# Scale and shift of a pre-norm moved from row operands to column operands, in a two-layer fp32 encoder

## The chip, the cores and the metric

One NeuronCore of a Trainium2 chip runs the whole program. The metric is device microseconds of one execution; the figure of a kernel is the median of several. In the profile the engines are PE (TensorE's matmuls), PEld (its weight loads), DVE (VectorE), ACT (ScalarE), POOL (GpSimd) and SP (SyncE, which issues the transfers).

## The reference

Two layers, 512 tokens, width 1024, fp32. Each layer has two sub-layers (a token mixer of four head groups, then a SwiGLU feed-forward of width 2816), each wrapped in the same way:

```
def _rms_norm(x, g, eps=RMS_EPS):
    y = xf * lax.rsqrt(jnp.mean(xf * xf, axis=-1, keepdims=True) + eps)
    return (y * g.astype(jnp.float32)).astype(x.dtype)

# per sub-layer, with shift, scale, gate taken from c by a linear layer:
h = _rms_norm(x, g_pre) * (1 + scale) + shift
x = x + gate * _rms_norm(sublayer(h), g_post)
```

So between two sub-layers, a token's row y of the finished sub-layer is normed, multiplied by a gate that differs per feature, added to x; the new x is normed again, multiplied per feature by S = (1 + scale) g_pre, and shifted per feature by H = shift. Gate, S and H depend on the feature and not on the token.

## The kernel before

Each fp32 product is made of three matmuls on parts: an operand is split into hi (rounded to the type fp32r) and lo (the rest), and mm3 issues hi·hi (L192), hi·lo (L193) and lo·hi (L194). The activations that feed a GEMM are kept transposed in hT: hT[:, 0] is hi, hT[:, 1] is lo, features on the 128 partitions in eight chunks kc, tokens along the row.

Between two sub-layers lies a **boundary**, in four tiles of 128 tokens, T0 to T3. There are four: b0 (mixer of layer 0 to its FFN, some 320 to 375 us into the span), b1 (FFN of layer 0 to the mixer of layer 1, some 715 to 765 us), b2 (mixer of layer 1 to its FFN, some 1000 to 1055 us) and a last one at the end, which has only the gate. The GEMM before a boundary leaves a tile's row y in two PSUM banks of 512 features each. boundary_tile then squares and sums the banks (L291 on ACT) and multiplies them by the gate row G (L293 on DVE); computes 1/rms from a few one-column instructions; adds the residual (L299); squares again (L303); and makes yt = x · r2 · S + H in two halves (L312 on DVE, then L313, the first half on POOL and the second on DVE). G, S and H are tiles in which one row of 1024 features is repeated on all 128 partitions. make_rows computes them as columns (rcol, 24 columns of 128 features), and cols_to_rows transposes them and writes them to DRAM; boundary_start reads them back as rows, 512 KB each, into three tiles of the pool FS. What remains of FS goes into the boundary's ring of buffers.

The function transposed() of a tile runs later: PE transposes yt in eight pieces of 128x128 (L319) back into the tile's own two banks, and split makes hi (L205, ACT) and lo (L206, DVE) from each bank of 512 columns, both reading the bank.

The next GEMM (FFN or mixer) can use T0 and T1 before T2 and T3 are there: it runs first on the tokens 0 to 255 (matmuls of 256 columns), the transposes of T2 and T3 are placed in between, then on the tokens 256 to 511. In b1 the 448-column value part (v_part, 48 matmuls of tokens 0 to 255) lies between T3's transposes and the first matmul that needs T3.

A scheduler orders the instructions of each engine when the kernel is built. Each engine executes its list in order, and an instruction that waits holds up what is behind it.

Of the kernel before, what the change touches and what calls it, by code (L numbers as in the profile page):

```python
# [16 lines left out]
A = mybir.AluOpType  # L17
AF = mybir.ActivationFunctionType
AX = mybir.AxisListType

L, D, T, FF = 2, 1024, 512, 2816
# [70 lines left out]
def f(ap):  # L92
    return ap.bitcast(F32)
# [3 lines left out]
def hybrid_encoder(ctx: ExitStack, tc: tile.TileContext, x_in, c_in, pos_in, cols_in, rows_in, ktab_in, wada, wz, wst,  # L97
# [5 lines left out]
    act, dve, pool, pe, sync = nc.scalar, nc.vector, nc.gpsimd, nc.tensor, nc.sync  # L103
# [3 lines left out]
    def persist(name, shape, dt=F32):  # L107
        t = sb.tile(shape, dt, name=name)
        tags[id(t)] = name
        return t  # L110
# [8 lines left out]
    hT = persist("hT", [128, 2, KC, T], F32R)  # L119
# [3 lines left out]
    FS = Pool2([persist(f"f{i}", [128, 1024]) for i in range(8)])  # L123
# [5 lines left out]
    rcol = persist("rcol", [128, 24])  # L129
# [10 lines left out]
    def small(n=1):  # L140
        s = state["s"]
        if s + n > 128:
            s = 0
        state["s"] = s + n
        return sml[:, s:s + n]

    x_mid = [dr.tile([T, D], F32, name=f"xmid{i}") for i in range(2 * L)]
    rows_d = [dr.tile([24, 128], F32, name=f"rowsd{i}") for i in range(2 * L)]
# [6 lines left out]
    def dram_ap(t, offset, ap):  # L155
        a = t[:] if not isinstance(t, bass.AP) else t
        return bass.AP(tensor=a.tensor, offset=a.offset + offset, ap=ap)
# [46 lines left out]
    def split(hi, lo, src):  # L204
        act.activation(hi, src, AF.Copy)  # L205
        dve.tensor_tensor(lo, src, f(hi), A.subtract)  # L206
# [7 lines left out]
    def col(l, c, n=8):  # L214
        return cols[:, l, c:c + n]

    def modcol(l, part):
        return mod[:, l, part * 8:part * 8 + 8]

    def add_bias(l, part):  # L220
        dve.tensor_tensor(modcol(l, part), modcol(l, part), col(l, C_BADA + part * 8), A.add)

    def make_rows(idx, ps, gate, pre):

        l, part, g = gate
        add_bias(l, part)
        dve.tensor_tensor(rcol[:, 0:8], modcol(l, part), col(l, g), A.mult)
        if pre:
            l, psc, psh, g = pre
            add_bias(l, psc)  # L230
            add_bias(l, psh)
            dve.scalar_tensor_tensor(rcol[:, 8:16], modcol(l, psc), 1.0, col(l, g), A.add, A.mult)
            dve.tensor_copy(rcol[:, 16:24], modcol(l, psh))
        n = 24 if pre else 8
        cols_to_rows(rcol[:, 0:n], n, rows_d[idx], ps)

    def rsqrt_col(ss, n):
        r = small()
        act.activation(r, ss, AF.Sqrt, bias=epst[:], scale=1.0 / n)
        dve.reciprocal(r, r)  # L240
        return r
# [12 lines left out]
    def cols_to_rows(c, n, d, ps):  # L254

        tmp = RAW.get()
        pe.transpose(ps[0:n, 0:128], c, ident[:])
        act.activation(tmp[0:n, 0:128], ps[0:n, 0:128], AF.Copy)
        sync.dma_start(d[0:n, :], tmp[0:n, 0:128])
        RAW.put(tmp)  # L260

    def boundary_start(idx, src, pre):
        st = {"idx": idx, "src": src, "pre": pre}
        names = ("G", "S", "H") if pre else ("G",)
        for i, nme in enumerate(names):
            st[nme] = FS.full()
            sync.dma_start(st[nme][:], dram_ap(rows_d[idx], i * D, [[0, 128], [1, D]]))
        st["scr"] = FS.half()
        st["junk"] = st["scr"][:, 0:256].bitcast(BF16)
        st["own"] = [FS.full() for _ in range(min(4, len(FS.full_free)))]  # L270
        st["raw"] = [RAW.get(), RAW.get()]
        st["ring"] = Ring(st["own"] + st["raw"] + ([cact] if idx else []))
        return st

    def boundary_end(st):
        for nme in ("G", "S", "H") if st["pre"] else ("G",):
            FS.put(st[nme])
        for t in st["own"]:
            FS.put(t)
        RAW.put(*st["raw"])  # L280
        FS.put_half(st["scr"])

    def boundary_tile(st, t, y, dst):

        xt, yt = st["ring"].get(), st["ring"].get()
        rows = slice(t * 128, t * 128 + 128)
        sync.dma_start(xt[:], st["src"][rows, :])
        ss = small(4)
        for e in range(2):
            h = slice(e * 512, e * 512 + 512)  # L290
            act.activation(st["junk"], y[e][:], AF.Square, accum_out=ss[:, e:e + 1])  # L291
            h = slice((1 - e) * 512, (1 - e) * 512 + 512)
            dve.tensor_tensor(yt[:, h], y[1 - e][:], st["G"][:, h], A.mult)  # L293
        s1 = small()
        dve.tensor_tensor(s1, ss[:, 0:1], ss[:, 1:2], A.add)
        r1 = rsqrt_col(s1, D)
        for e in range(2):
            h = slice(e * 512, e * 512 + 512)
            dve.scalar_tensor_tensor(xt[:, h], yt[:, h], r1, xt[:, h], A.mult, A.add)  # L299
            if not st["pre"] and t == NT - 1:  # L300
                sync.dma_start(dst[rows, h], xt[:, h])
            if st["pre"]:
                act.activation(st["junk"], xt[:, h], AF.Square, accum_out=ss[:, 2 + e:3 + e])  # L303
        if st["pre"] or t < NT - 1:
            sync.dma_start(dst[rows, :], xt[:])
        if st["pre"]:
            s2 = small()
            dve.tensor_tensor(s2, ss[:, 2:3], ss[:, 3:4], A.add)
            r2 = rsqrt_col(s2, D)
            for e in range(2):  # L310
                h = slice(e * 512, e * 512 + 512)
                dve.scalar_tensor_tensor(yt[:, h], xt[:, h], r2, st["S"][:, h], A.mult, A.mult)  # L312
                (pool, dve)[e].tensor_tensor(yt[:, h], yt[:, h], st["H"][:, h], A.add)  # L313
        st["ring"].put(xt)

        def transposed():
            for e in range(2):
                for k in range(4):
                    pe.transpose(y[e][:, k * 128:k * 128 + 128], yt[:, e * 512 + k * 128:e * 512 + k * 128 + 128], ident[:])  # L319
                src = y[e][:].rearrange("p (k t) -> p k t", k=4)  # L320
                split(hT[:, 0, e * 4:e * 4 + 4, rows], hT[:, 1, e * 4:e * 4 + 4, rows], src)
            st["ring"].put(yt)

        st[t] = transposed
# [306 lines left out]
    def mixer(l, tile2=None):  # L631
# [55 lines left out]
        else:  # L687
            zb, vb = [bank[i] for i in (0, 4, 1, 5)], [bank[i] for i in (2, 6, 3, 7)]
            us = env.pop("us") + [load_unit(wst[l, kc], 960, True) for kc in range(EARLY, KC)]
            for half in range(2):  # L690
                for j in range(4):
                    for kc in range(KC):
                        z_part(zb[j], us[kc], j, kc, half * 256, half * 256 + 256)
                    if half == 0 and j == 0:
                        tile2(0)[0][2]()
                if half == 0:
                    tile2(0)[0][3]()
                    boundary_end(tile2(0)[0])
                for t in (2 * half, 2 * half + 1):
                    for kc in range(KC):  # L700
                        v_part(vb[t], us[kc], t, kc)
# [500 lines left out]
    def ffn(l, yb, st, us, rows, tile2):  # L1202
# [14 lines left out]
        for half in range(2):  # L1217
            for n, (ug, uu, pg, pu) in enumerate(us):
                gemm_z(pg, ug, half * 256, half * 256 + 256)
                if half == 0 and n == 0:  # L1220
                    st[2]()
                gemm_z(pu, uu, half * 256, half * 256 + 256)
            if half == 0:
                st[3]()
                boundary_end(st)
# [30 lines left out]
    for l in range(L):  # L1256
        b = L * 4 + l * 128
        lam_init = 0.8 - 0.6 * math.exp(-0.3 * l)
        e = small(2)
# [47 lines left out]
    src = x_in  # L1307
    for l in range(L):
# [3 lines left out]
        st = {}  # L1312

        def rows1():
            make_rows(2 * l, yb[3][1], (l, 2, C_GQM), (l, 4, 3, C_GPF))
            st.update(boundary_start(2 * l, src, True))

        def tile1(t):
            boundary_tile(st, t, yb[t], dst)
# [10 lines left out]
        src2, src = dst, out if last else x_mid[2 * l + 1]  # L1330
        st2 = {}

        def tile2(t, l=l, src2=src2, src=src, st2=st2, last=last):
            if not st2:
                st2.update(boundary_start(2 * l + 1, src2, not last))
            return st2, t, (bank[t], bank[4 + t]), src

        ffn(l, yb, st, us, lambda ps: make_rows(2 * l + 1, ps, (l, 5, C_GQF), None if last else (l + 1, 1, 0, C_GPM)), tile2)


# [79 lines left out]
```

## Time and profile before

| | us |
|---|---|
| median of 3 runs | 1412.16 (1410.44 to 1414.13) |
| profiled execution | 1408.21 |
| its span, first to last instruction | 1406.4 |
| PE busy | 1316.7 (94%) |
| DVE busy | 822.9 (59%) |
| ACT busy | 609.2 (43%) |
| POOL busy | 157.4 (11%) |

The span covers one execution from its first to its last instruction; busy time is what an engine's instructions took, overlapped ones counted once. The mean clock granted to TensorE was 0.976 of full speed.

### The profile page before, as it was taken

How to read it: one execution, taken by the hardware profiler on the slowest of the kernel's cores; microseconds unless marked ns; L12 is line 12 of the kernel's file. 1: busy time of each engine (PE TensorE's matmuls, PEld its weight loads, DVE VectorE, ACT ScalarE, POOL GpSimd, SP SyncE). 2: the span in 40 equal slices, each digit the busy share in tenths (PEclk: the TensorE clock that was granted, in tenths of full speed). 3: DMA queues.
4: the chain of work that ended last, by engine and by line, in shares of the span. 5: the costliest groups of instructions: out<-in, count | busy, mean ns of one | idle time of the engine just before them, and what ended most of it. 6: DMA issues, size and time to landing. Idle time of an engine off the chain costs nothing. (4 is left out here: it accounts for less than half of the span.)

```text
span 1406.4 us, 17870 instructions
## 1 busy us (share of the span) xinstructions
PE 1316.7 (94%) x6512; PEld 1090.2 (78%) x6512; DVE 822.9 (59%) x1562; ACT 609.2 (43%) x1163; POOL 157.4 (11%) x156
## 2 busy tenths in 40 slices
PE   4989899899999999999989998999989999999998
PEld 4857777677888887778869787777878888888886
DVE  6969887886665556542274597778574333332223
ACT  6555555765422222232252575677543223232212
POOL 0223332111000000000031112211010000000000
PEclk9989899999999999999999999999999999999999
DMA  8776786736476666663344533653553233323321
GB/s 314 258 193 205 256 255 207 220 114 222 147 245 215 215 217 226 225 225 90 105 139 143 150 108 107 181 152 109 183 175 120 90 105 90 105 105 125 100 90 60
DMA packets 80324, 231.69 MB, mean 165 GB/s; under 512 B 11276, under 2 KB 12268, under 8 KB 80236
## 3 DMA queue, kind: packets, MB, share of 16 engines
q1 hardware_dynamic: 80236, 230.55, 51.1%
q8 instruction: 51, 0.84, 0.2%
q14 instruction: 37, 0.30, 0.1%
HBM read 188.85 MB, written 14.40 MB: 145 GB/s over the span
## 5 line engine op out<-in xcount | busy, mean ns | idle before, releaser
L192 PE MATMUL bank<-hT,w 128*128 128x512 f32 (+1 forms) x992 | 376.3, 381 | 12.6 <-ACT hT L1299 4.0
L194 PE MATMUL bank<-hT,w 128*128 128x512 f32 (+1 forms) x992 | 376.7, 380 | 4.1 <-DVE w L183 3.3
L193 PE MATMUL bank<-hT,w 128*128 128x512 f32 (+1 forms) x992 | 377.4, 381 | 2.1 <-DVE hT L206 2.1
L178 ACT ACTIVATE w<-r 128x1024 fp32r<-128x1024 f32 (+1 forms) x132 | 138.4, 1056 | 329.1 <-PE bank L194 111.1
L183 DVE TENSOR_TENSOR w<-r,w 128x1024 fp32r<-128x1024 f32 (+1 forms) x102 | 124.5, 1222 | 238.1 <-ACT w L178 238.1
L192 PEld LDWEIGHTS bank<-hT,w 128*128 128x128 f32 x992 | 189.6, 192 | 48.2 <-ACT w L178 4.9
L194 PEld LDWEIGHTS bank<-hT,w 128*128 128x128 f32 x992 | 190.2, 192 | 40.1 <-DVE w L183 6.3
L193 PEld LDWEIGHTS bank<-hT,w 128*128 128x128 f32 x992 | 190.2, 192 | 34.8 <-DVE hT L206 2.9
L192 PE MATMUL bank<-w,r 128*128 128x512 f32 (+1 forms) x312 | 122.2, 392 | 1.6 <-DVE r L206 0.8
L194 PE MATMUL bank<-w,r 128*128 128x512 f32 (+1 forms) x312 | 121.2, 389 | 1.1 <-DVE r L206 1.1
L193 PE MATMUL bank<-w,r 128*128 128x512 f32 (+1 forms) x312 | 120.7, 387 | 0.0
L178 ACT ACTIVATE w<-raw 128x1024 fp32r<-128x1024 f32 (+1 forms) x48 | 50.3, 1051 | 121.4 <-PE bank L194 42.6
L211 DVE SCALAR_TENSOR_TENSOR r<-r,cact 128x1024 f32<-128x1024 f32 x69 | 84.6, 1227 | 28.4 <-DMA r<-in_wada_dram 27.4
L485 PE MATMUL bank<-ident,f 128*128 128x128 f32 x464 | 76.0, 285 | 11.4 <-DVE f L461 4.5
L205 ACT ACTIVATE r<-bank 128x512 fp32r<-128x512 f32 (+3 forms) x121 | 61.2, 513 | 48.9 <-PE bank L485 31.9
L183 DVE TENSOR_TENSOR w<-raw,w 128x1024 fp32r<-128x1024 f32 (+1 forms) x38 | 46.1, 1213 | 55.4 <-ACT w L178 55.4
L485 PEld LDWEIGHTS bank<-ident,f 128*128 128x128 f32 x464 | 55.3, 145 | 27.6 <-ACT f L440 7.5
L192 PEld LDWEIGHTS bank<-w,r 128*128 128x128 f32 x312 | 58.7, 188 | 15.7 <-DVE r L206 1.4
L194 PEld LDWEIGHTS bank<-w,r 128*128 128x128 f32 x312 | 58.7, 188 | 13.4 <-DVE r L206 1.6
L206 DVE TENSOR_TENSOR r<-bank,r 128x512 fp32r<-128x512 f32 (+3 forms) x89 | 49.9, 568 | 32.0 <-ACT r L205 31.6
L180 POOL TENSOR_TENSOR w<-r,w 128x512 fp32r<-128x512 f32 (+1 forms) x30 | 45.2, 1505 | 208.9 <-ACT w L178 156.9
L193 PEld LDWEIGHTS bank<-w,r 128*128 128x128 f32 x312 | 58.8, 188 | 11.5
(399 smaller groups left out, 2171.4 us busy)
## 6 DMA issues: line engine op xcount, KB each, us to landing
r<-in_wada_dram SPq DMA_DIRECT2D x69, 512.0 KB
r<-in_wgu_dram SPq DMA_DIRECT2D x66, 512.0 KB
r<-in_wdn_dram SPq DMA_DIRECT2D x33, 512.0 KB
raw<-in_wada_dram SPq DMA_DIRECT2D x27, 512.0 KB
raw<-in_wgu_dram SPq DMA_DIRECT2D x22, 512.0 KB
r<-r SPq DMA_DIRECT2D x35, 256.0 KB
r<-in_wz_dram SPq DMA_DIRECT2D x17, 512.0 KB
r<-w SPq DMA_DIRECT2D x66, 128.0 KB
```

The lines of the kernel that those rows point to most:

```text
L178: act.activation(hi[:, :w], raw[:, :w], AF.Copy)
L180: pool.tensor_tensor(lo[:, :w // 2], raw[:, :w // 2], f(hi[:, :w // 2]), A.subtract)
L183: dve.tensor_tensor(lo[:, :w], raw[:, :w], f(hi[:, :w]), A.subtract)
L192: pe.matmul(ps, a[0], b[0], start=start, stop=False)
L193: pe.matmul(ps, a[0], b[1], start=False, stop=False)
L194: pe.matmul(ps, a[1], b[0], start=False, stop=stop)
L205: act.activation(hi, src, AF.Copy)
L206: dve.tensor_tensor(lo, src, f(hi), A.subtract)
L211: dve.scalar_tensor_tensor(raw[:], raw[:], 1.0, cact[:], A.mult, A.mult, accum_out=mod[:, l, e:e + 1])
L485: pe.transpose(tb[:, s], P[:, s], ident[:])
```

## The change

Only G goes to DRAM and comes back as a row: 8 columns instead of 24 are transposed, and one row tile of 512 KB is loaded per boundary instead of three. The two tiles of FS that held S and H join the boundary's ring. boundary_tile now makes yt = x · r2 in one instruction of 1024 columns. S and H are applied after the transposes, when features lie on partitions: per piece of 128 columns, ACT writes hi = bank · s + h straight from the bank (s and h are columns of rcol), DVE computes the same value in fp32 from the bank into the buffer yt, and per 512 columns one more DVE instruction subtracts hi from it to give lo.

```diff
-        n = 24 if pre else 8
-        cols_to_rows(rcol[:, 0:n], n, rows_d[idx], ps)
+        cols_to_rows(rcol[:, 0:8], 8, rows_d[idx], ps)
...
-        names = ("G", "S", "H") if pre else ("G",)
-        for i, nme in enumerate(names):
-            st[nme] = FS.full()
-            sync.dma_start(st[nme][:], dram_ap(rows_d[idx], i * D, [[0, 128], [1, D]]))
+        st["G"] = FS.full()
+        sync.dma_start(st["G"][:], dram_ap(rows_d[idx], 0, [[0, 128], [1, D]]))
...
-            for e in range(2):
-                h = slice(e * 512, e * 512 + 512)
-                dve.scalar_tensor_tensor(yt[:, h], xt[:, h], r2, st["S"][:, h], A.mult, A.mult)
-                (pool, dve)[e].tensor_tensor(yt[:, h], yt[:, h], st["H"][:, h], A.add)
+            dve.tensor_scalar(yt[:], xt[:], r2, None, A.mult)
...
-                src = y[e][:].rearrange("p (k t) -> p k t", k=4)
-                split(hT[:, 0, e * 4:e * 4 + 4, rows], hT[:, 1, e * 4:e * 4 + 4, rows], src)
+                for k in range(4 * e, 4 * e + 4):
+                    ps, s, h = y[e][:, (k % 4) * 128:(k % 4) * 128 + 128], rcol[:, 8 + k:9 + k], rcol[:, 16 + k:17 + k]
+                    act.activation(hT[:, 0, k, rows], ps, AF.Identity, bias=h, scale=s)
+                    dve.tensor_scalar(yt[:, k * 128:k * 128 + 128], ps, s, h, A.mult, A.add)
+                dve.tensor_tensor(hT[:, 1, e * 4:e * 4 + 4, rows], yt[:, e * 512:e * 512 + 512].rearrange("p (k t) -> p k t", k=4),
+                                  f(hT[:, 0, e * 4:e * 4 + 4, rows]), A.subtract)
```

Line numbers of the changed kernel that the prediction uses: the scaling by r2 is L306; PE's transposes are L312; ACT's pieces are L315, DVE's L316, the subtraction L317; the old L293 is L289 and the old L299 is L295.

The scheduler lists the instructions anew. On DVE, at the end of T3 in b0 (its banks are bank_66 and bank_70; f_108 and f_111 are buffers of yt), before:

```order
L312 SCALAR_TENSOR_TENSOR f_108<-raw_102,sml,f_107 128x512 x2
L313 TENSOR_TENSOR f_108<-f_108,f_110 128x512
L206 TENSOR_TENSOR hT<-bank_66,hT 128x4x128
L206 TENSOR_TENSOR hT<-bank_70,hT 128x4x128
L183 TENSOR_TENSOR w_73<-r_163,w_72 128x1024
```

and after the change, from T3's L306 on, which stands among T2's pieces (f_110 and bank_69 are T2's), with the waits that the program holds in brackets (the waiting semaphore's number left as printed):

```order
L306 TENSOR_SCALAR f_111<-f_108,sml 128x1024 [waits DVE_49]
L316 TENSOR_SCALAR f_110<-bank_69,rcol 128x128 [waits Activation_49] x3
L317 TENSOR_TENSOR hT<-f_110,hT 128x4x128 [waits DVE_49]
L316 TENSOR_SCALAR f_111<-bank_66,rcol 128x128 [waits Activation_49]
L316 TENSOR_SCALAR f_111<-bank_70,rcol 128x128 [waits Activation_49]
L316 TENSOR_SCALAR f_111<-bank_66,rcol 128x128 [waits Activation_49]
```

Five more L316 follow, the two banks still in turn, and then T3's two L317: the two instructions behind T3's transposes became ten. Each L316 waits for ACT, as the brackets show, although it reads nothing that ACT writes; in ACT's list each L315 but the first of a bank waits for DVE in the same way. The two engines go through a bank piece by piece in turn, on two banks at once.

On PE, where the first GEMM behind b0 begins, T1's transposes (banks 64 and 68) are followed before by the GEMM, with T2's transposes (bank_65) 49 matmuls later:

```order
L319 MATMUL bank_64<-ident,f_108 128x128 x4
L319 MATMUL bank_68<-ident,f_108 128x128 x4
L192 MATMUL bank_63<-hT,w_72 128x256
L192 MATMUL bank_67<-hT,w_75 128x256
L193 MATMUL bank_63<-hT,w_72 128x256
```

and after the change T2's eight stand ahead of the GEMM's first L193:

```order
L312 MATMUL bank_64<-ident,r_165 128x128 x4
L312 MATMUL bank_68<-ident,r_165 128x128 x4
L192 MATMUL bank_63<-hT,w_72 128x256
L192 MATMUL bank_67<-hT,w_75 128x256
L312 MATMUL bank_65<-ident,f_110 128x128 x4
L312 MATMUL bank_69<-ident,f_110 128x128 x4
L192 MATMUL bank_64<-hT,w_1589 128x256
L193 MATMUL bank_63<-hT,w_72 128x256
```

T2's transposes moved ahead; in b2 it is the same, and in b1 T2's eight and four of T3's stand there. T3's eight stay behind some 94 matmuls of 256 columns in b0 and b2.

On DVE in b1, the work ahead of T1's L317 (which the mixer's first L193 waits for) now holds the pieces of T0 and T1, and some of T2's chain; this is its middle part (f_109 is T1's buffer, r_165 T2's, cact and r_2919 T3's):

```order
L289 TENSOR_TENSOR r_2919<-bank_66,f_108 128x512
L317 TENSOR_TENSOR hT<-r_2920,hT 128x4x128
L316 TENSOR_SCALAR r_2920<-bank_67,rcol 128x128
L291 TENSOR_TENSOR sml<-sml 128x1
L316 TENSOR_SCALAR f_109<-bank_64,rcol 128x128
L317 TENSOR_TENSOR hT<-r_2920,hT 128x4x128
L239 RECIPROCAL sml<-sml 128x1
L316 TENSOR_SCALAR f_109<-bank_68,rcol 128x128
L295 SCALAR_TENSOR_TENSOR cact<-r_2919,sml,cact 128x512
L295 SCALAR_TENSOR_TENSOR cact<-r_2919,sml,cact 128x512
L316 TENSOR_SCALAR f_109<-bank_64,rcol 128x128
```

T3's L289 and L295, the old L293 and L299, now stand between T1's pieces.

## Rows read from the trace of the kernel before

**Rows 1.** The page: span and busy time of each engine.

```profile
span 1406.4 us, 17870 instructions
PE 1316.7 (94%) x6512; PEld 1090.2 (78%) x6512; DVE 822.9 (59%) x1562; ACT 609.2 (43%) x1163; POOL 157.4 (11%) x156
```

**Rows 2.** Groups of PE by shape: busy us, mean ns, idle before, its releasers.

```profile
L319 PE MATMUL bank<-ident,f 128*128 128x128 f32 x48 | 7.2, 281 | 5.1 <-POOL f L313 3.9 <-DVE sml L240 1.1
L319 PE MATMUL bank<-ident,r 128*128 128x128 f32 x40 | 5.9, 274 | 1.0 <-POOL r L313 1.0
```

**Rows 3.** Timeline of PE in b0, b1, b2: start, us, instruction, [idle before <-releaser].

```profile
350.25 1.34 PE L319 MATMUL bank<-ident,f 128*128 128x128 f32 x8 [1.36 <-POOL f L313]
352.97 0.58 PE L193 MATMUL bank<-hT,w 128*128 128x256 f32 x1 [0.87 <-DVE hT L206]
...
369.70 1.27 PE L319 MATMUL bank<-ident,f 128*128 128x128 f32 x8 [1.66 <-POOL f L313]
371.77 0.38 PE L193 MATMUL bank<-hT,w 128*128 128x256 f32 x1
...
737.58 0.80 PE L192 MATMUL bank<-hT,r 128*128 128x256 f32 x2 [2.73 <-ACT hT L205]
...
1030.40 1.32 PE L319 MATMUL bank<-ident,cact 128*128 128x128 f32 x8 [0.30 <-POOL cact L313]
...
1035.37 0.58 PE L193 MATMUL bank<-hT,w 128*128 128x256 f32 x1 [1.26 <-DVE hT L206]
```

**Rows 4.** Windows: length, busy PE, PEld, DVE, ACT, POOL, clock, DMA share, GB/s.

```profile
718.50:738.20 19.70, 14.95 (x70) 11.40 (x68) 17.96 (x30) 10.92 (x30) 6.22 (x4) 0.91 0.20 70
353.00:359.00 6.00, 6.00 (x28) 6.00 (x29) 4.44 (x11) 3.19 (x10) 0.76 (x1) 0.50 0.22 87
1030.00:1035.40 5.40, 1.91 (x12) 1.17 (x11) 5.00 (x10) 3.19 (x8) 0.34 (x1) 0.96 0.29 83
1035.40:1038.40 3.00, 3.00 (x14) 3.00 (x15) 2.36 (x6) 1.08 (x5) 0.77 (x1) 0.51 0.56 227
```

**Rows 5.** Groups of ACT by shape.

```profile
L291 ACT ACTIVATE f<-bank 128x512 bf16<-128x512 f32 x24 | 14.2, 593 | 33.1 <-DVE r L293 30.2 <-PE bank L194 1.7 <-DVE f L293 0.9
L334 ACT ACTIVATE r<-bank 128x512 fp32r<-128x512 f32 x9 | 5.3, 592 | 4.1 <-DVE w L206 1.9 <-issue 1.3 <-PE bank L415 0.7
L334 ACT ACTIVATE r<-bank,kcst 128x512 fp32r<-128x512 f32 x5 | 3.4, 687 | 4.7 <-PE bank L194 4.3 <-DVE r L211 0.3
L205 ACT ACTIVATE r<-bank 128x128 fp32r<-128x128 f32 x4 | 1.1, 280 | 0.4 <-DVE r L206 0.2
```

**Rows 6.** Groups of DVE by shape.

```profile
L206 DVE TENSOR_TENSOR hT<-bank,hT 128x512 fp32r<-128x512 f32 x24 | 15.9, 684 | 7.0 <-ACT hT L205 6.8
L335 DVE SCALAR_TENSOR_TENSOR r<-bank,r 128x512 fp32r<-128x512 f32 x9 | 6.2, 686 | 0.6 <-ACT r L334 0.6
L313 DVE TENSOR_TENSOR r<-r,f 128x512 f32<-128x512 f32 x4 | 5.7, 1418 | 0.0
L312 DVE SCALAR_TENSOR_TENSOR r<-f,sml,f 128x512 f32<-128x512 f32 x6 | 4.2, 748 | 0.1
L335 DVE SCALAR_TENSOR_TENSOR r<-bank,kcst,r 128x512 fp32r<-128x512 f32 x5 | 3.7, 747 | 0.9 <-ACT r L334 0.9
L1281 DVE TENSOR_SCALAR f<-f,sml 128x1024 f32<-128x1024 f32 x4 | 3.0, 752 | 0.1
L206 DVE TENSOR_TENSOR r<-bank,r 128x128 fp32r<-128x128 f32 x4 | 1.2, 288 | 0.1
```

**Rows 7.** Timeline of DVE and ACT, at T0 and T3 of b0.

```profile
328.30 1.29 DVE L293 TENSOR_TENSOR r<-bank,f 128x512 f32<-128x512 f32 x2 [2.90 <-DMA f<-rowsd]
...
329.08 0.60 ACT L291 ACTIVATE f<-bank 128x512 bf16<-128x512 f32 x1 [4.95 <-DVE r L293]
...
370.40 1.21 ACT L205 ACTIVATE hT<-bank 128x512 fp32r<-128x512 f32 x2 [3.51 <-PE bank L319]
...
371.02 1.31 DVE L206 TENSOR_TENSOR hT<-bank,hT 128x512 fp32r<-128x512 f32 x2 [0.83 <-ACT hT L205]
```

More of the change, by code (lines that the diff above doesn't have):

```diff
@@ L275, in boundary_end @@
     def boundary_end(st):
-        for nme in ("G", "S", "H") if st["pre"] else ("G",):
-            FS.put(st[nme])
+        FS.put(st["G"])
         for t in st["own"]:
```

## The prediction

> **What bounds the kernel now.** First the page: PE is busy 94% of the span, DVE 59%, ACT 43%, POOL 11% [rows 1]. A change that leaves PE's work alone (its 96 boundary transposes of 128x128 stay) can then act only where PE waits. So next the groups of PE's transposes, which show these waits: 5.1 us before those from f buffers and 1.0 us before those from r buffers, mostly for POOL's L313 [rows 2]. Last the timeline of PE in the boundaries, which shows the second kind of wait, that of the GEMM for hT. In b0 T1's transposes start at 350.25 after 1.36 us of idleness, and the GEMM's first L193, which needs lo, at 352.97; T3's start at 369.70 after 1.66 us, and the next L193 at 371.77, 2.07 us later [rows 3]. In b1 the first L192 waits 2.73 us for ACT's hi, and in b2 the first L193 stands at 1035.37 [rows 3]. The windows say what else runs there: ahead of b1's GEMM DVE is busy 17.96 of 19.70 us, so that DVE sets when it starts; and after a stretch in which PE was busy 1.91 of 5.40 us (b2's gate) the clock granted to PE was 0.51 for the next 3 us, and 0.50 for 6 us in b0 [rows 4]. [...]
>
> **What goes.** Two row loads of 512 KB per boundary and 16 columns of a small store. DMA was busy a fifth of the time in b1's window [rows 4]; DVE waited 2.90 us for a row at T0 of b0 [rows 7], but for G, the first row, which stays. I take nothing for the loads; the bound is these 2.9 us in one place, and PE then works on the earlier GEMM's last matmuls for T1 to T3, which hide T0's chain. In each tile two L312 of .748 and the L313 pair of about 1.42 [rows 6] become one L306. The trace has the same form at the start of the program, 128x1024 by a column, .752 [rows 6]. The chain to the transposes shortens from 2.9 us (two L312, then L313 on POOL and DVE at once) to .75, about 2.1 us. That removes the waits of up to 1.66 us ahead of the transposes.
>
> **What comes.** Per bank, one L205 (.60) and one L206 (.684, [rows 6, 7]) become four L315, four L316 and one L317. The trace does not have these forms, so from their neighbours: ACT from a bank, 128x128, takes .280; a column as scale adds .095 (.687 against .592 for 128x512) [rows 5], and with two columns L315 is about .47. DVE from a bank, 128x128, takes .288; a column adds .061 (.747 against .686) [rows 6], so L316 is about .41. L317 is priced as L206, .68. The lower bound is .28 for either (columns free), the upper .60 and .68 (a piece as dear as a whole bank).
>
> L315 and L316 of one bank wait for each other by the program's own semaphores. The trace has such a turn: ACT's L291 and DVE's L293 both only read a bank, and ACT sat idle 30.2 us before L291 for DVE [rows 5]. A hand-over costs .1 from DVE to ACT (the second half of L293 begins .60 after 328.30 and the first ends about .68 after it; L291 begins at 329.08) and .02 the other way (L205 ends .60 after 370.40, L206 begins at 371.02) [rows 7]. A pair is thus .47 + .02 + .41 + .10 = 1.00, four are 4.0 us per bank, and two banks go on side by side, since each engine is busy less than half of a pair.
>
> [...]
>
> **T3's tail** (b0 and b2). Counted from the start of T3's transposes: .65 until the first bank's four are through (half of 1.27), 4.0 for its pieces, .4 for the other bank's last L316, which DVE has ahead of L317, .68 for L317, .1 to PE: 5.8 against 2.07 [rows 3]. So +3.75 each. In b0 the wait of 1.66 ahead of T3's transposes goes, since the shorter chain ends while PE is still at the 256-column matmuls: +2.1. For b2 I take all, +3.75. b1 costs nothing: 48 matmuls of 448 columns lie behind T3's last transposes, and 28 matmuls of 256 columns took 6.00 us at half clock [rows 4], so 48 hide at least 5.1 us. Without that cover b1 would pay the same 3.75.
>
> **The gate of the first GEMM.** It is T1's first L317 now. In b0 T1's transposes can start at 348.8 (350.25 less the wait and a little). Then .65 to the first bank, DVE's work up to that L317 (seven L316 2.3, two L289 at .60 each 1.2, T2's L306 .67, L317 of T0 and of T1 1.3, small ones .3: 5.7 in all) and .85 for turns in which DVE waits for ACT: 7.2 us, L193 at 356.0 against 352.97, +3.05. T2's eight transposes are done in that gap; they would have cost 1.27 − .28 = 1.0 later. Net +2.05. In b2 T1's transposes can start 1.6 us before 1030.40, since the chain ends earlier: 1028.8 + 7.2 = 1036.0 against 1035.37, less 1.0, −.35.
>
> In b1 DVE is full [rows 4], so what is put ahead of T1's L317 comes out as time. There stand now, over before: eighteen L316 at .33 (.41 less .08 of overlap, as two L293 take 1.29 and not 1.37) 5.9, four L306 2.7, two more halves of the residual 1.3 (priced as L312), one more L293 and one L181 .6 each, six one-column instructions .5; less four L312 2.7 and two L313 2.7. In sum +6.2, less 1.5 for the twelve transposes done early: +4.7. Behind DVE's waiting instructions are T3's residual and norm and the splits of the mixer's first weights; nobody else waits for these before the gate.
>
> **Clock.** T3's tail leaves PE busy some 2 of 5.8 us, as in the window ahead of b2's gate, after which the clock stood at 0.51 for 3 us [rows 4]: half of it lost, 1.5 each in b0 and b2, +3.0. Bounds: 0 (the clock stayed up after T3's 2-us tail) and 3.0 each (as in b0's 6 us).
>
> **Sum.** b0 2.05 + 2.1, b1 4.7, b2 −.35 + 3.75, clock 3.0: +15.3. The profiled execution took 1408.2, so 1423.5; the median shown is 4.0 above it, which makes 1427. With every term low it is +4: pairs of .7 (tails +2.55, so .9 in b0), no turn waits at the gates (1.2 and −1.2), b1 +.5, no loss of clock. The high end is C, below, +24.
>
> **The rivals.** *A, faster.* The tile's chain is 2.1 us shorter, and the bound sits in that chain: PE waited for L313 and its like about 6.1 us [rows 2] and for the gates some 5 us more [rows 3]. If a pair of pieces costs about half of what I take (some .5, the engines reading side by side), hi and lo come as soon as they did, b1's +6.2 shrinks to about 3 less what the chain gives back, and what remains is the saved waiting and the clock kept up behind it: about −8, 1404. The point that decides is the pair: at about .6 us the sum is nothing. Against it: two durations of .28 are .56 without any column or hand-over [rows 5, 6]. Chance .07.
>
> *B, no change.* The terms lie at their low ends and the shorter chain pays for the rest: gates in b0 and b2 earlier by the 1.6 us, tails partly hidden because the L192 with hi go ahead. Against it: four turns per bank cannot be under 2.2 us, where two instructions did it before. 1412 to 1416. Chance .13.
>
> *C, slower still.* Behind each new gap the clock stays down as long as in 353 to 359, and b1's saturated DVE makes ACT late too, which then holds up the next pair: hand-overs of .2 both ways, pairs of 1.28, tails of +4.9 (3.2 net in b0), gates as above, b1 8, the clock 6: 2.05 + 3.2 + 8 − .35 + 4.9 + 6 = +24, 1436. For it speaks that ACT was idle 30 us for DVE in just these places. Chance .12.
>
> **How the numbers follow.** My case holds .68, C .12, B .13, A .07. The likeliest is 1427. The range takes in the low sum (1412 + 4, and the upper part of B) and nearly all of C: 1414 to 1436; A, the lower half of B and the far end of C stay out, about 2 in 10. A measurement of this kernel tells some 0.3%, 4 us, from no change: faster is A, .07; same B with the very lowest end of mine, .13; slower the rest, .80.
>
> **What would show it.** L306 near .75, twelve times; 96 L315 near .47 and 96 L316 near .41, most with an idle time before them that ends on the other engine; L193 5 to 6 us after T3's transposes in b0 and b2; T1's wait for L313 gone; the first L193 in b0 about 3 and in b1 about 6 us later than now; the clock at 0.5 for some us after T3's tails; outside the boundaries nothing. I am wrong if pieces overlap on one bank, if a piece is nearer .28 than .45, or if b1's delay does not come out because its chain, freed of L312 and L313, starts earlier.

## The result and the profile after

The changed kernel took 1430.36 us (median of four, 1424.24 to 1434.04) beside 1412.93 of the kernel before: a ratio of 1.0129, 95% interval 1.0103 to 1.0154. A second set of five (after_again) gave 1432.82 beside 1411.22, and 1.0154 (1.0136 to 1.0172). The forecast was 1427, in a range of 1414 to 1436. The profiled execution took 1424.24 us, 16.0 more than the one of before. From the page, and from the groups of PE by shape (busy us, mean ns, idle before, its releasers), which answer to [rows 1] and [rows 2]:

```profile
span 1422.4 us, 17965 instructions
PE 1321.1 (93%) x6512; PEld 1094.3 (77%) x6512; DVE 834.5 (59%) x1634; ACT 633.9 (45%) x1235; POOL 134.9 (9%) x144
```

```profile
L193 PE MATMUL bank<-hT,w 128*128 128x256 f32 x144 | 44.9, 314 | 8.0 <-DVE hT L317 8.0
...
L192 PE MATMUL bank<-hT,w 128*128 128x256 f32 x144 | 43.8, 314 | 1.4 <-DVE r L316 1.0
...
L312 PE MATMUL bank<-ident,r 128*128 128x128 f32 x48 | 8.4, 309 | 12.0 <-DVE r L306 12.0
L312 PE MATMUL bank<-ident,f 128*128 128x128 f32 x40 | 5.2, 274 | 2.6 <-DVE f L306 2.6
...
L312 PE MATMUL bank<-ident,cact 128*128 128x128 f32 x8 | 1.9, 421 | 3.2 <-DVE cact L306 3.2
```

PE's waits ahead of its transposes did not go: 17.8 us now (12.0 + 2.6 + 3.2), for L306. And 8.0 us stand ahead of L193, for L317. The timeline of PE in b0, b1 and b2 says where, beside [rows 3]:

```profile
351.60 1.09 PE L312 MATMUL bank<-ident,f 128*128 128x128 f32 x8 [2.57 <-DVE f L306]
...
354.20 0.58 PE L193 MATMUL bank<-hT,w 128*128 128x256 f32 x1 [0.53 <-DVE hT L317]
...
368.03 1.03 PE L312 MATMUL bank<-ident,f 128*128 128x128 f32 x8
...
373.47 0.39 PE L193 MATMUL bank<-hT,w 128*128 128x256 f32 x1 [3.55 <-DVE hT L317]
...
735.37 1.63 PE L312 MATMUL bank<-ident,r 128*128 128x128 f32 x7 [4.88 <-DVE r L306]
...
745.29 0.48 PE L312 MATMUL bank<-ident,r 128*128 128x128 f32 x1 [7.07 <-DVE r L306]
...
746.70 0.56 PE L193 MATMUL bank<-hT,r 128*128 128x256 f32 x1
...
1042.63 1.91 PE L312 MATMUL bank<-ident,cact 128*128 128x128 f32 x8 [3.20 <-DVE cact L306]
...
1046.02 0.58 PE L193 MATMUL bank<-hT,w 128*128 128x256 f32 x1 [0.40 <-DVE hT L317]
...
1058.83 1.03 PE L312 MATMUL bank<-ident,f 128*128 128x128 f32 x8
...
1064.27 0.58 PE L193 MATMUL bank<-hT,w 128*128 128x256 f32 x1 [3.55 <-DVE hT L317]
```

T3's transposes (368.03, 1058.83) are followed by L193 5.44 us later in both boundaries. The longest of the other waits are those of T2's and T3's transposes, which now stand ahead of the first GEMM. That GEMM's first L193 came at 738.30 in b1 of the kernel before; the two of b0 and b2 are in [rows 3]:

```profile
738.30 0.58 PE L193 MATMUL bank<-hT,r 128*128 128x256 f32 x1
```

To see what each boundary lost, the same matmul (the k-th that is no boundary transpose) is looked up in both traces, ahead of the boundary and behind it. Starts in us:

| | before | after | shift | the boundary |
|---|---|---|---|---|
| ahead of b0 | 335.14 | 333.79 | −1.35 | |
| behind b0 | 390.18 | 393.37 | +3.19 | +4.5 |
| ahead of b1 | 715.04 | 713.46 | −1.58 | |
| behind b1 | 764.04 | 770.64 | +6.60 | +8.2 |
| ahead of b2 | 1010.19 | 1019.42 | +9.23 | |
| behind b2 | 1060.03 | 1075.90 | +15.87 | +6.6 |

The boundaries lost 19.4 us (4.5, 8.2 and 6.6). Between b0 and b1 this execution won 4.8 back, in good part in the FFN, where PE of the kernel before had waited 5.4 us for the splits of weights (L178 and L183, in 390 to 713 us) and waits 1.6 here, and between b1 and b2 it lost 2.6. Neither stretch is touched by the change, and in the profiled execution of the second set the two shifts are +1.3 and −0.3; so boundaries are compared below.

The groups of ACT and DVE by shape give the new instructions, of which the trace before had only neighbours [rows 5, 6]:

```profile
L315 ACT ACTIVATE hT<-bank,rcol 128x128 fp32r<-128x128 f32 x96 | 40.7, 456 | 33.9 <-PE bank L312 22.6 <-DVE r L316 4.0 <-DVE f L316 3.5
```

```profile
L316 DVE TENSOR_SCALAR r<-bank,rcol 128x128 f32<-128x128 f32 x48 | 18.2, 404 | 9.0 <-ACT hT L315 8.7
L316 DVE TENSOR_SCALAR f<-bank,rcol 128x128 f32<-128x128 f32 x40 | 15.8, 405 | 13.5 <-ACT hT L315 12.6
...
L306 DVE TENSOR_SCALAR f<-f,sml 128x1024 f32<-128x1024 f32 x3 | 2.2, 748 | 0.0
```

And T3's tail in b0, first DVE's timeline, then ACT's:

```profile
369.16 3.65 DVE L316 TENSOR_SCALAR f<-bank,rcol 128x128 f32<-128x128 f32 x8 [5.99 <-ACT hT L315]
372.73 1.28 DVE L317 TENSOR_TENSOR hT<-f,hT 128x512 fp32r<-128x512 f32 x2
```

```profile
368.67 3.70 ACT L315 ACTIVATE hT<-bank,rcol 128x128 fp32r<-128x128 f32 x8 [6.67 <-PE bank L312]
```

Eight pieces take 3.65 us on DVE and 3.70 on ACT, side by side: .46 for each piece on both engines. The turn of the two does not stand in these rows as idle time; it stands in the length of the group. Without turns, DVE does six in 2.00 us (dve_reads) and ACT eight in 2.90 (act_first).

The clock behind the tails of b0 and b2, two windows of the changed kernel for each (columns as in [rows 4]):

```profile
373.30:376.30 3.00, 2.83 (x14) 2.84 (x15) 0.71 (x2) 0.00 (x0) 0.00 (x0) 0.57 0.28 87
376.30:380.00 3.70, 3.70 (x30) 3.70 (x30) 1.01 (x1) 2.09 (x2) 0.00 (x0) 0.89 0.00 0
...
1064.00:1069.00 5.00, 4.73 (x22) 4.73 (x23) 0.81 (x2) 0.00 (x0) 0.00 (x0) 0.50 0.00 0
1069.00:1074.00 5.00, 5.00 (x40) 5.00 (x40) 2.31 (x3) 4.43 (x5) 0.00 (x0) 0.90 0.23 53
```

### The profile page after: what moved, and what is told of

It is laid out like the page before. It is cut to its first block, busy times and chain, and to the rows that moved or that the text cites. A ratio compares the mean times of both kernels' runs of the same rounds, so it can differ in the third digit from the quotient of the medians.

```text
span 1422.4 us, 17965 instructions
## 1 busy us (share of the span) xinstructions
PE 1321.1 (93%) x6512; PEld 1094.3 (77%) x6512; DVE 834.5 (59%) x1634; ACT 633.9 (45%) x1235; POOL 134.9 (9%) x144
## 5 line engine op out<-in xcount | busy, mean ns | idle before, releaser
L192 PE MATMUL bank<-hT,w 128*128 128x512 f32 (+1 forms) x992 | 377.7, 383 | 10.1 <-ACT hT L1296 4.0
L193 PE MATMUL bank<-hT,w 128*128 128x512 f32 (+1 forms) x992 | 378.1, 381 | 8.0 <-DVE hT L317 8.0
L178 ACT ACTIVATE w<-r 128x1024 fp32r<-128x1024 f32 (+1 forms) x132 | 138.4, 1055 | 328.3 <-PE bank L194 111.3
L183 DVE TENSOR_TENSOR w<-r,w 128x1024 fp32r<-128x1024 f32 (+1 forms) x102 | 124.5, 1221 | 238.6 <-ACT w L178 238.6
L192 PEld LDWEIGHTS bank<-hT,w 128*128 128x128 f32 x992 | 191.0, 193 | 45.3 <-ACT hT L1296 4.3
L193 PEld LDWEIGHTS bank<-hT,w 128*128 128x128 f32 x992 | 192.1, 194 | 40.8 <-DVE hT L317 9.0
L192 PE MATMUL bank<-w,r 128*128 128x512 f32 (+1 forms) x300 | 117.6, 392 | 1.9 <-ACT f L1205 0.8
L194 PE MATMUL bank<-w,r 128*128 128x512 f32 (+1 forms) x300 | 116.6, 389 | 0.0
L193 PE MATMUL bank<-w,r 128*128 128x512 f32 (+1 forms) x300 | 116.1, 387 | 0.0
L178 ACT ACTIVATE w<-raw 128x1024 fp32r<-128x1024 f32 (+1 forms) x48 | 50.3, 1050 | 121.0 <-PE bank L194 43.9
L183 DVE TENSOR_TENSOR w<-raw,w 128x1024 fp32r<-128x1024 f32 (+1 forms) x38 | 46.1, 1214 | 56.0 <-ACT w L178 55.9
L192 PEld LDWEIGHTS bank<-w,r 128*128 128x128 f32 x300 | 56.5, 188 | 15.4 <-DVE r L206 1.4
L180 POOL TENSOR_TENSOR w<-r,w 128x512 fp32r<-128x512 f32 (+1 forms) x30 | 45.4, 1512 | 227.9 <-ACT w L178 205.5
L194 PEld LDWEIGHTS bank<-w,r 128*128 128x128 f32 x300 | 56.6, 189 | 11.8 <-DVE r L206 0.4
L193 PEld LDWEIGHTS bank<-w,r 128*128 128x128 f32 x300 | 56.6, 189 | 11.1
L482 PE MATMUL bank<-ident,f 128*128 128x128 f32 x304 | 50.5, 289 | 10.0 <-DVE f L458 3.8
L501 PE MATMUL bank<-r,r 128*128 128x256 f32 x288 | 53.6, 301 | 5.8 <-ACT r L205 4.9
```

Source lines behind the costliest of these rows:

```text
L178: act.activation(hi[:, :w], raw[:, :w], AF.Copy)
L180: pool.tensor_tensor(lo[:, :w // 2], raw[:, :w // 2], f(hi[:, :w // 2]), A.subtract)
L183: dve.tensor_tensor(lo[:, :w], raw[:, :w], f(hi[:, :w]), A.subtract)
L192: pe.matmul(ps, a[0], b[0], start=start, stop=False)
L193: pe.matmul(ps, a[0], b[1], start=False, stop=False)
L194: pe.matmul(ps, a[1], b[0], start=False, stop=stop)
```

## The experiments

The first theory is the prediction's: the pieces cost, since ACT and DVE take turns at a bank, and hi and lo come late. Its rivals: the transposes of T2 and T3 that the scheduler put ahead of the first GEMM block PE; it is the amount of work on an engine and not the turns; the loads and buffers matter. All kernels are variants of the changed one unless said otherwise. Ratios are against the kernel before on the same chip, with 95% intervals.

**order_kept.** PE's transposes are tied behind the matmuls that they followed before, in all three boundaries:

```diff
...
                 if half == 0 and n == 0:
-                    st[2]()
+                    with tc.issue_after(nc.cur_bb.bb.instructions[-1]):
+                        st[2]()
...
```

> The changed kernel with PE's transposes of T2 and T3 tied behind the matmuls that they stood behind in the kernel before (issue order on PE only). VectorE's and ScalarE's lists stay almost the same. In the changed kernel PE waits 2.57, 4.88, 7.07 and 3.20 us ahead of these transposes for L306. Theory 1 (the pieces on VectorE and ScalarE set the gate, so T1's lo is late anyway): those waits turn into waits of the first L193 for L317, and the time stays within 3 us of the changed kernel, about 1428. Theory 2 (the hoisted transposes block PE, the pieces matter little): 10 us or more come back, about 1417 or less, and in b1 the first L193 stands some 7 us earlier.

1430.71 us, ratio 1.015 (1.0129 to 1.017): nothing came back. The groups of PE show the waits in another place:

```profile
L193 PE MATMUL bank<-hT,w 128*128 128x256 f32 x144 | 45.0, 315 | 8.0 <-DVE hT L317 8.0
...
L192 PE MATMUL bank<-hT,w 128*128 128x256 f32 x144 | 43.3, 310 | 10.0 <-DVE r L316 9.2 <-ACT hT L315 0.5
L192 PE MATMUL bank<-hT,r 128*128 128x256 f32 x48 | 15.0, 317 | 13.0 <-DVE f L316 7.3 <-DVE r L316 5.6
L312 PE MATMUL bank<-ident,r 128*128 128x128 f32 x48 | 6.2, 272 | 0.0
```

and in PE's timeline of b1 the longest of them:

```profile
750.60 0.90 PE L192 MATMUL bank<-hT,r 128*128 128x256 f32 x2 [7.34 <-DVE f L316]
```

The 17.8 us ahead of the transposes became 23.0 ahead of L192, nearly all for L316: the first matmuls write into the banks of T0 and T1, and these are free only when all pieces of them have been read. The first L193 comes at 751.51, as soon as the first of T1's two L317 is through, which are next on DVE:

```profile
750.77 1.29 DVE L317 TENSOR_TENSOR hT<-f,hT 128x512 fp32r<-128x512 f32 x2
```

```profile
751.51 0.58 PE L193 MATMUL bank<-hT,r 128*128 128x256 f32 x1
```

The hoisted transposes fill a wait; they don't make it. Theory 1 holds, this rival falls.

**no_pieces.** The old split of 512 columns stands in place of the pieces; S and H are left out of the computation. What is left is L306, one row load of three and the two buffers.

```diff
-                for k in range(4 * e, 4 * e + 4):
...
+                src = y[e][:].rearrange("p (k t) -> p k t", k=4)
+                split(hT[:, 0, e * 4:e * 4 + 4, rows], hT[:, 1, e * 4:e * 4 + 4, rows], src)
```

> The changed kernel with the old split of 512 columns per bank in place of the pieces; S and H are left out of the computation altogether. What remains of the change is the one L306 per tile, one row load of three, and the two more buffers. Theory 1 (the pieces cost everything): faster than the kernel before, 1404 to 1410, since the chain to the transposes is 2 us shorter and PE's waits for L313 go. Theory 2 (the transposes hoisted on PE cost): still 1416 or more, since T2's transposes stand ahead of the first GEMM here too.

1398.92 us, ratio 0.9927 (0.9905 to 0.9949), more than was expected. Although T2's transposes stand ahead of the GEMM here too, they wait little:

```profile
L312 PE MATMUL bank<-ident,r 128*128 128x128 f32 x48 | 7.2, 295 | 0.3 <-DVE r L306 0.3
L312 PE MATMUL bank<-ident,f 128*128 128x128 f32 x40 | 5.4, 274 | 0.5 <-DVE f L306 0.5
```

So what is left of the change, loads and buffers included, is worth some 10 to 12 us, and the pieces cost 29 to 32 (ratios of 1.0129 and 1.0154 against 0.9927).

**act_first.** The same pieces on the same engines; on each bank ACT's four are written first, then DVE's four.

```diff
-                for k in range(4 * e, 4 * e + 4):
-                    ps, s, h = y[e][:, (k % 4) * 128:(k % 4) * 128 + 128], rcol[:, 8 + k:9 + k], rcol[:, 16 + k:17 + k]
-                    act.activation(hT[:, 0, k, rows], ps, AF.Identity, bias=h, scale=s)
+                kk = [(k, y[e][:, (k % 4) * 128:(k % 4) * 128 + 128], rcol[:, 8 + k:9 + k], rcol[:, 16 + k:17 + k]) for k in range(4 * e, 4 * e + 4)]
+                for k, ps, s, h in kk:
+                    act.activation(hT[:, 0, k, rows], ps, AF.Identity, bias=h, scale=s)
+                for k, ps, s, h in kk:
                     dve.tensor_scalar(yt[:, k * 128:k * 128 + 128], ps, s, h, A.mult, A.add)
```

> The changed kernel with the same pieces on the same engines, only written in another order: on each bank first ScalarE's four, then VectorE's four, so that the two engines change over once per bank and not eight times. Theory 1a (the turns cost): L193 4.7 us after T3's transposes start in place of 5.4, the gates lose most turn waits, 1416 to 1424. Theory 1b (only the work of the engines costs, which is the same here): 1427 to 1433.

1419.2 us, ratio 1.0053 (1.0029 to 1.0077), as theory 1a has it. T3's tail in b0, on PE and on ACT:

```profile
370.33 1.03 PE L312 MATMUL bank<-ident,f 128*128 128x128 f32 x8
374.97 0.58 PE L193 MATMUL bank<-hT,w 128*128 128x256 f32 x1 [2.75 <-DVE hT L318]
```

```profile
370.97 2.90 ACT L315 ACTIVATE hT<-bank,rcol 128x128 fp32r<-128x128 f32 x8 [5.93 <-PE bank L312]
```

L193 comes 4.64 us after the transposes begin (expected 4.7; 5.44 with the turns), and ACT's eight pieces take 2.90 in place of 3.70. The change of one loop's order gave back some 0.75 to 1% of the time. T2's transposes were hoisted less far in b0 and T3's not at all in b1, which by order_kept is no cause. But in b1 more changed than the turns. T2's and T3's residuals (two L295 each) took 2.37 and 2.96 us in the changed kernel, beside one and two of POOL's L180; here POOL's instructions run at other times, and the pairs take 1.41 and 1.40. First the changed kernel (T3's row is shown at the end), then act_first:

```profile
728.57 2.37 DVE L295 SCALAR_TENSOR_TENSOR r<-r,sml,r 128x512 f32<-128x512 f32 x2
```

```profile
735.96 1.41 DVE L295 SCALAR_TENSOR_TENSOR r<-r,sml,r 128x512 f32<-128x512 f32 x2
...
744.45 1.40 DVE L295 SCALAR_TENSOR_TENSOR cact<-r,sml,cact 128x512 f32<-128x512 f32 x2
```

So up to 2.5 us of what act_first gave back may be this and not the turns.

**dve_reads** and **act_reads.** One engine alone reads the banks. In the first DVE writes yt, and hi and lo come from it, 512 columns each; in the second ACT writes each piece twice, as hi and as fp32, and DVE only subtracts.

```diff
-                    act.activation(hT[:, 0, k, rows], ps, AF.Identity, bias=h, scale=s)
                     dve.tensor_scalar(yt[:, k * 128:k * 128 + 128], ps, s, h, A.mult, A.add)
-                dve.tensor_tensor(hT[:, 1, e * 4:e * 4 + 4, rows], yt[:, e * 512:e * 512 + 512].rearrange("p (k t) -> p k t", k=4),
-                                  f(hT[:, 0, e * 4:e * 4 + 4, rows]), A.subtract)
+                split(hT[:, 0, e * 4:e * 4 + 4, rows], hT[:, 1, e * 4:e * 4 + 4, rows],
+                      yt[:, e * 512:e * 512 + 512].rearrange("p (k t) -> p k t", k=4))
```

```diff
                     act.activation(hT[:, 0, k, rows], ps, AF.Identity, bias=h, scale=s)
-                    dve.tensor_scalar(yt[:, k * 128:k * 128 + 128], ps, s, h, A.mult, A.add)
+                    act.activation(yt[:, k * 128:k * 128 + 128], ps, AF.Identity, bias=h, scale=s)
```

> The changed kernel, but only VectorE reads the banks: eight pieces of 128 columns per tile into yt, then hi by ScalarE and lo by VectorE from SBUF, 512 columns each. VectorE's work stays the same (eight pieces and two of 512 per tile), ScalarE's is 8 x 0.46 less 2 x 0.62 smaller. Theory 1a (the turns of the two engines at a bank cost the tail): L193 comes about 3.6 us after T3's transposes and not 5.4, 2 us less in each of b0 and b2, and the gates lose the turn waits: 1418 to 1423. Theory 1b (the amount of VectorE's work costs, not the turns): 1426 to 1430, with the tail near 5.

1414.77 us, ratio 1.0038 (1.0019 to 1.0057): better than theory 1a had it. The tail in b0, on PE and DVE:

```profile
366.81 1.03 PE L312 MATMUL bank<-ident,f 128*128 128x128 f32 x8
369.53 0.74 PE L192 MATMUL bank<-hT,w 128*128 128x256 f32 x4 [1.69 <-ACT hT L205]
```

```profile
367.45 2.00 DVE L315 TENSOR_SCALAR f<-bank,rcol 128x128 f32<-128x128 f32 x6 [3.51 <-PE bank L312]
```

PE waits for hi now, and after the four L192 (.74) nothing more: L193 some 3.5 us after the transposes begin. By the same look-up as above b0 is 3.1 us shorter than in the kernel before, b1 4.5 and b2 2.5 longer.

> The changed kernel, but only ScalarE reads the banks: each piece is written twice, as hi and as fp32, 16 pieces of 0.46 us per tile; VectorE keeps the subtraction alone and loses 96 pieces of 0.40 us. No turns. Theory 1a (turns): 1414 to 1422 although ScalarE's boundary work doubles. Theory 1c (what matters is that VectorE is relieved or not): in b1 the gate is no later than in the kernel before, 1412 or less. If the longer row of pieces on one engine costs as much as the turns: 1426 or more.

1420.73 us, ratio 1.0059 (1.0035 to 1.0083), with ACT's boundary pieces doubled and no turns: theory 1a. That VectorE's relief alone matters (1412 or less) is wrong: b1 is 4.7 us longer than before here too.

**rows_loaded** and **after_again.** In the first all 24 columns go through DRAM and the rows S and H are loaded into their buffers, unread; the second is the changed kernel once more.

```diff
-        cols_to_rows(rcol[:, 0:8], 8, rows_d[idx], ps)
+        n = 24 if pre else 8
+        cols_to_rows(rcol[:, 0:n], n, rows_d[idx], ps)
...
-        st["G"] = FS.full()
-        sync.dma_start(st["G"][:], dram_ap(rows_d[idx], 0, [[0, 128], [1, D]]))
+        for i, nme in enumerate(("G", "S", "H") if pre else ("G",)):
+            st[nme] = FS.full()
+            sync.dma_start(st[nme][:], dram_ap(rows_d[idx], i * D, [[0, 128], [1, D]]))
...
```

> The changed kernel with all 24 columns sent through DRAM and the rows S and H loaded into their two buffers as before, but not read. If the loads and buffers are worth nothing, as forecast: within 3 us of the changed kernel, 1427 to 1433. If fewer loads and two more ring buffers hid part of the loss: 1435 or more.

> The changed kernel itself, on the chip of the next two, as the yardstick: 1426 to 1432, 1.2 to 1.5% over the kernel before.

With the rows loaded: 1436.72 us, ratio 1.0147 (1.0115 to 1.0178), beside 1.0129 and 1.0154 (1.0136 to 1.0172, 1432.82 us) of the changed kernel. By the ratios this is no difference, by the bare time it is the rival's 1435. In its trace the three boundaries are 28.4 us longer than in the kernel before, in the two traces of the changed kernel 19.4 and 21.4; some 5 us of that difference lie in b0, where the scheduler ordered VectorE's list differently. So having fewer loads and more buffers may be worth some us to the changed kernel; how much is not shown.

**early_s**, **early_s_again.** The kernel before, with x·S computed while ACT squares x, so that only one instruction per half follows 1/rms; POOL has no part.

```diff
+            for e in range(2):
+                h = slice(e * 512, e * 512 + 512)
+                dve.tensor_tensor(yt[:, h], xt[:, h], st["S"][:, h], A.mult)
             s2 = small()
...
-                dve.scalar_tensor_tensor(yt[:, h], xt[:, h], r2, st["S"][:, h], A.mult, A.mult)
-                (pool, dve)[e].tensor_tensor(yt[:, h], yt[:, h], st["H"][:, h], A.add)
+                dve.scalar_tensor_tensor(yt[:, h], yt[:, h], r2, st["H"][:, h], A.mult, A.add)
```

> The kernel before, with x*S computed on VectorE while ScalarE squares x, so that behind 1/rms only two instructions are left per tile (times 1/rms plus H) and POOL has no part: the chain to the transposes is about 1.4 us shorter, the split stays as it was. If the bound of the boundaries is the token-side chain, as the 6.4 us of waits ahead of the transposes say, 2 to 5 us come off the kernel before: 1408 to 1411. If the two extra products get in the way of VectorE's other work in b1, no change: 1412 to 1414.

> The kernel early_s once more: 0.1 to 0.4% below the kernel before if its gain is real (its three boundaries were 2.1, 1.2 and 1.1 us shorter in the trace), no change if the first result was chance.

1407.4 us, ratio 0.9977 (0.9961 to 0.9992), and again 1407.58, 0.9966 (0.9948 to 0.9984): a little faster than the kernel before, and both intervals leave out 1. PE's waits ahead of the transposes [rows 2] are gone:

```profile
L321 PE MATMUL bank<-ident,f 128*128 128x128 f32 x48 | 6.2, 272 | 0.0
L321 PE MATMUL bank<-ident,r 128*128 128x128 f32 x40 | 5.8, 287 | 0.0
```

**diag**, **diag_order**, **diag_four.** S early as a row; the transpose becomes a product with identity times 1/rms; H is added to a whole bank by one DVE instruction that reads its column for all tokens; then the split from SBUF.

```diff
-                    pe.transpose(y[e][:, k * 128:k * 128 + 128], yt[:, e * 512 + k * 128:e * 512 + k * 128 + 128], ident[:])
+                    pe.matmul(y[e][:, k * 128:k * 128 + 128], yt[:, e * 512 + k * 128:e * 512 + k * 128 + 128], st["dg", t], start=True, stop=True)
...
+                dve.tensor_tensor(g, y[e][:].rearrange("p (k t) -> p k t", k=4), bass.AP(tensor=hc.tensor, offset=hc.offset, ap=[hc.ap[0], [1, 4], [0, 128]]), A.add)
```

> A candidate: S is multiplied in early as a row (while ScalarE squares x), 1/rms goes into the matrix that PE multiplies by for the transpose (identity times 1/rms, 128x128), and H is added behind it by one VectorE instruction per bank of 512 with the column read for all 128 tokens; then the split from SBUF. The chain from 1/rms to the transposes falls from 1.5 (early_s) to about 0.2 us; a bank's tail grows by 0.7. If the token-side chain bounds: 1399 to 1404, below early_s. If the added instruction at the tail and the order that the scheduler finds eat it: 1407 or more.

> The kernel diag with PE's transposes tied to the places that they have in the kernel before; in diag the scheduler had put T0's transposes of b1 behind T3's last matmuls, where they waited 4.94 us. Its b0 and b2 were 3.0 and 2.6 us shorter than before, its b1 4.7 longer. If the order is b1's whole loss: 5 to 8 us below the kernel before, 1403 to 1407. If the instruction added at each bank is the loss: 1409 or more.

> The kernel diag with four matrices of identity times 1/rms in place of two that take turns. In diag and diag_order T2's and T3's matrices overwrote T0's and T1's in b1 ahead of their transposes, so that these used another tile's 1/rms and had to wait for it. Without that, b1 should lose its wait of 4.94 us and T0's and T1's transposes stand where they were before. With b0 and b2 as in diag (3.0 and 2.6 us shorter than the kernel before) and b1 within 1 us of before: 1404 to 1408, as good as early_s or better. If the added instruction per bank costs b1 as much as the pieces did without turns (dve_reads: 4.5 us): 1410 or more.

diag took 1409.03 us, 0.9975 (0.9957 to 0.9993), not the 1399 to 1404 that were hoped for. In it, and in diag_order, two matrices took turns, and in b1 T0 and T1 were transposed with the 1/rms of T2 and T3. That made T0's transposes wait for T2's chain, and the expectation for diag_order, which took the order for the cause, was wrong: tied to its place, PE stood 7.98 us for it, 1425.3 us, 1.0107 (1.009 to 1.0125). PE's timeline in b1 of diag_order:

```profile
731.38 3.50 PE L320 MATMUL bank<-r,f 128*128 128x128 f32 x16 [7.98 <-DVE r L314]
```

diag_four, with four matrices, has no such mistake: 1406.87 us, 0.9972 (0.9954 to 0.999). It is as fast as early_s; b0 and b2 are 2.6 and 2.4 us shorter than before, b1 2.1 longer. early_s is the simpler one.

The three boundaries of each variant, by the same look-up, in us against the kernel before. It is one execution each; the first two rows show how far two of one kernel differ.

| | b0 | b1 | b2 | together |
|---|---|---|---|---|
| changed kernel | +4.5 | +8.2 | +6.6 | +19.4 |
| after_again | +4.7 | +8.7 | +8.1 | +21.4 |
| order_kept | +4.0 | +8.4 | +8.4 | +20.8 |
| no_pieces | −6.6 | −1.0 | −4.1 | −11.6 |
| act_first | +2.4 | +3.2 | +4.8 | +10.4 |
| dve_reads | −3.1 | +4.5 | +2.5 | +3.9 |
| act_reads | +1.2 | +4.7 | +1.6 | +7.4 |
| rows_loaded | +9.5 | +10.0 | +9.0 | +28.4 |

## Why the prediction was right

The time lies 3 us above the forecast, that of the second set 6, and the mechanism is the forecast one: the token-side chain got shorter, and the short pieces with their turns cost more than that gave. That the two profiled executions differ by 16.0 us, next to the 15.3 of the sum, is luck: the boundaries lost 19.4, and this execution won 3.4 outside them.

- **Prices.** L306 .748 for .75; L315 .456 for .47; L316 .405 for .41. The neighbours' rows with a column's surcharge were enough. Where DVE runs alone, it takes .33 from one piece to the next (2.00 us for six, dve_reads), the figure of b1's sum. The pair of a turn was .91 (3.65 us for eight pieces on two banks) for 1.00.
- **T3's tails.** 5.44 us for 5.8 in b0 and b2; against the kernel before's 2.07, +3.4 for +3.75. PE's wait ahead of T3's transposes in b0 went, as forecast. b1's tail cost nothing, as forecast.
- **Clock.** The granted clock was 0.57 and then 0.89 in the two windows behind b0's tail, 0.50 and then 0.90 in those behind b2's; behind b0's tail of the kernel before it was 1.00 (371.80 to 376.00 us). The share that is missing, times the length, comes to 1.7 and 3.0 us, for 1.5 each. The forecast is right in kind and 1.7 too low.
- **The gates, one by size wrong.** A boundary's change has two parts. The first ends at the GEMM's first L193: how much later that comes than before, less the shift ahead of the boundary. The second is what lies behind it (tail, clock, transposes done early). In us:

| | b0 | b1 | b2 |
|---|---|---|---|
| up to the first L193, forecast | +3.05 | +6.2 | +0.65 |
| measured | +2.6 | +10.0 | +1.4 |
| behind it, forecast | +2.6 | −1.5 | +4.25 |
| measured | +2.0 | −1.8 | +5.2 |

So the term that was mis-sized is b1's gate, by 3.8 us; b2's miss is mostly its clock. That T1's first L317 sets the gate was right: L193 waits for it to the end in b0 and b2, and in b1 it comes at 746.70, some .2 us after the first of T1's two is through:

```profile
745.79 1.28 DVE L317 TENSOR_TENSOR hT<-f,hT 128x512 fp32r<-128x512 f32 x2
```

PE stands in its queue before that, at T2's and T3's transposes or, in order_kept, at the L192 that writes into T1's bank (7.34), but these waits end before that L317 does. What the sum had too low was the time that DVE takes for its list ahead of L317. From the matmul ahead of b1 to the first L193, first all engines (columns as in [rows 4]), then the residual's instructions on DVE alone (length, busy DVE, clock, DMA share, GB/s), before and after:

```profile
715.04:738.30 23.26, 18.51 (x85) 14.28 (x83) 19.97 (x34) 14.17 (x35) 7.85 (x5) 0.92 0.26 93
715.04:738.30 23.26, 4.22 (x6) 0.92 0.26 93
```

```profile
713.46:746.70 33.24, 21.07 (x100) 17.13 (x98) 27.71 (x59) 24.78 (x64) 6.89 (x5) 0.83 0.39 147
713.46:746.70 33.24, 8.16 (x8) 0.83 0.39 147
```

DVE works 7.7 us more, for 6.2, and is idle 2.2 us more (5.5 for 3.3), for which b1's sum had nothing. Of the work, the residual grew by 3.9 for the 1.3 forecast ("two more halves"): the pairs of T2 and T3 ran beside POOL. The other terms of the work came out some 1.1 lower together.

- **Turns.** With one change-over per bank (act_first) the ratio is 1.0053, some 7.5 us, and with one reader 1.0038 and 1.0059. So of the changed kernel's 17 to 22 us over before, 10 to 14 went with the turns; up to 2.5 of them may be b1's residual beside POOL (act_first). Only 14 of the 96 L315 and 13 of the 96 L316 have an idle time before them that ends on the other engine, where the prediction had expected most; the turns stand in the length of the groups. The program's waits keep the two engines apart at a bank; no run here tried what they do there without these.
- **Rival A** named a gain that is there: no_pieces shows 10 to 12 us without the pieces. Its condition, pieces half as dear, didn't come true.

What stays open: how DVE's idle time in b1 divides between the turns and ACT's other work; what b1 would be with POOL's instructions elsewhere and nothing else changed, since no run moved them alone; and what the two row loads are worth.

## What to carry to other kernels

A factor per partition needs no row tile, but here it cut an instruction of 512 columns (.60 us on ACT, .684 on DVE [rows 6, 7]) into four (.456 and .405 each), and with two engines at one bank the pieces took turns, .46 us each, beside .36 (ACT in act_first) and .33 (DVE in dve_reads) without turns. Write the loop so that one engine finishes a bank before the other begins, or let one engine read it alone and take the rest from SBUF: here the change of that order was worth some 0.75 to 1% of the time, with what it did to the engines' lists. And when a list is ordered anew, look at what now runs beside what: four residual instructions that stood beside POOL's took 2.5 us more in b1 than where they did not. Look, too, for what can be computed before the last scalar is known: x·S ahead of 1/rms gave 0.2 to 0.3% with no new tail.

## What the runs showed of the hardware

In T3's tail a turn of ACT and DVE piece by piece shows no idle time in the rows, only a longer group: eight ACT pieces 3.70 us in turns, 2.90 without (act_first).

DVE's timeline, and POOL's beside it, in b1 of the changed kernel:

```profile
739.47 2.96 DVE L295 SCALAR_TENSOR_TENSOR cact<-r,sml,cact 128x512 f32<-128x512 f32 x2
```

```profile
738.94 1.27 POOL L180 TENSOR_TENSOR w<-raw,w 128x512 fp32r<-128x512 f32 x1 [6.42 <-ACT w L178]
740.42 1.46 POOL L180 TENSOR_TENSOR w<-r,w 128x512 fp32r<-128x512 f32 x1 [0.21 <-ACT w L178]
```

Two DVE instructions that read two operands from SBUF and take about .75 each alone [rows 6], or 1.40 as a pair (act_first), took 2.96 together while POOL's ran; the pair ends .55 us behind the second of POOL's. The four instructions of this form, the pair among them, have a mean of 1132 ns here and of 1134 in the second set's trace, beside 749 in dve_reads. L181 of DVE, which also reads two operands from SBUF, took 1.69, 1.68 and 1.52 us where a POOL L180 had begun .19 or .20 before it (703.65, 709.09 and 731.51 in the changed kernel), and .66 where it began .04 ahead of one (705.39, 710.97 and 715.94); these three L180 took 1.69 or 1.70, the other three 1.20 to 1.37. In all six the instruction of each kind was longer where it began later; what held it is not shown.
